# A count scan whose zero operand lies in PSUM, and a result store moved back in the queue of loads

## The chip, the cores and the metric

The kernel runs on one core of a Trainium2 chip. Times are device microseconds of one whole execution; lower is better. A profile gives the *span* of one profiled execution, which in these runs is mostly 1.8 to 2.3 us shorter than the time of the same execution. So times are compared with times here, and spans with spans.

## The reference

```python
# x: 8 x 2048 x 4096, w: 4096 x 1, float32
proj = (x @ w).squeeze(-1)
cm = np.maximum.accumulate(proj, axis=1)
is_record = (proj >= cm).astype(np.float32)
return np.cumsum(is_record, axis=1)
```

A projection of 16384 rows, and for each of 8 batches a running maximum, a compare and a running count over 2048 positions. The input is 268 MB, the output 64 KB.

## The kernel before

Positions 0 to 1919 are handled in five groups of 384 positions for all 8 batches (the loop); the last 128 positions form the *last batch*, which is cut into rows and smaller pieces so that little is left to do when the last data land. VectorE multiplies and sums columns 0 to 2815 of each row, GpSimd multiplies the remaining 1280 columns, and ScalarE sums GpSimd's products. TensorE transposes the sums into the tile `ps` in PSUM, and VectorE runs three instructions on them, the scans. The kernel places its tiles in two memories, SBUF and PSUM: `ps` and `w_v` lie in PSUM, the other tiles in SBUF. A *dot* below is one VectorE instruction that multiplies a row by w and sums.

```python
    ends = cut(2)                                   # two columns of an SBUF tile
    neg, zero = ends[:B, 0:1], ends[:B, 1:2]
    ...
    def scans(cm_, rec_, cnt_, n, cm0, cnt0):
        V.tensor_tensor_scan(                       # running maximum: PSUM and SBUF
            out=cm_, data0=ps[:B, :n], data1=neg.to_broadcast([B, n]), initial=cm0,
            op0=ALU.max, op1=ALU.max,
        )._wait_ge(psr, 1).then_inc(psr, 1)
        V.tensor_tensor(                            # compare: PSUM and SBUF
            out=rec_, in0=ps[:B, :n], in1=cm_, op=ALU.is_ge
        )._wait_ge(psr, 2).then_inc(psr, 1)
        V.tensor_tensor_scan(                       # count: SBUF and SBUF
            out=cnt_, data0=rec_, data1=zero.to_broadcast([B, n]), initial=cnt0,
            op0=ALU.add, op1=ALU.add,
        )._wait_ge(psr, 3).then_inc(cs, 1)
    ...
        for m, b in enumerate(rows):                # last batch: six rows ...
            row_load(m, 0, D, b, xt[m])
            if m == 3:                              # result of the fifth group
                SY.dma_start(
                    out=out[:, (NG - 1) * N : S0], in_=cnt
                )._wait_ge(cs, NG).then_inc(oe, 16)
        for i, (b, c0, c1, _, _) in enumerate(PIECES):   # ... and eight pieces
            row_load(B - 1 - b, c0, c1, b, xq[i])
    ...
        def piece(xb, v, p, dst_v, dst_p, landed):
            dot(xb[:, v[0] : v[1]], w_v[:, v[0] : v[1]], dst_v)._wait_ge(
                landed, 16).then_inc(sd, 1)         # VectorE, w in PSUM
            ...
            if p:
                xl = xb[:, p[0] : p[1]]
                G.tensor_mul(out=xl, in0=xl, in1=w_pool(*p))._wait_ge(
                    landed, 16).then_inc(pl, 1)     # GpSimd, both inputs in SBUF
                add_up(xl, dst_p)._wait_ge(pl, npool).then_inc(pa, 1)   # ScalarE
```

All loads and stores of x and the result are issued in program order by one queue (SyncE), so a store that waits holds up every load behind it (in the profile below a store waits for 36.9 us and is issued at 602.74, and the next load at 603.09). GpSimd does not take part in the scans: when it has finished its part of the fifth group it goes on to the last batch, while VectorE still has the fifth group's scans to do.

## Time and profile before

| | before |
|---|---|
| median of the first three timed runs | 632.62 us (632.54, 634.55, 632.62) |
| the profiled execution | 635.03 us, span 632.9 us |
| DMA | 90% busy or more in 39 of 40 slices, mean 424 GB/s |
| VectorE, GpSimd busy | 64%, 58% |
| fifth count scan | 3.74 us (the other four: 1.005 us) |

Loads bound most of the span. The change concerns the last 35 us. This is the timeline of the kernel before around the fifth group's scans and at the last dot. Columns: start in us, length in us, engine, source line, operation, output<-input, shapes, count, and in brackets the idle time before it with what ended it. DVE is VectorE, POOL is GpSimd, PE is TensorE, ACT is ScalarE, and SPq is the queue of loads and stores.

```profile
...
595.93 2.90 POOL L285 TENSOR_TENSOR xall<-xall,w_sb 128x1280 f32<-128x1280 f32 x1
...
597.35 1.00 DVE L132 TENSOR_TENSOR_SCAN cm<-ps,cm,small 8x384 f32<-8x384 f32 x1 [3.58 <-PE ps L264]
...
598.97 3.74 DVE L139 TENSOR_TENSOR_SCAN cnt<-rec,cnt,small 8x384 f32<-8x384 f32 x1
598.99 2.91 POOL L285 TENSOR_TENSOR xall<-xall,w_sb 128x1280 f32<-128x1280 f32 x1 [0.17 <-DMA xall<-in_x_dram]
...
602.64 3.05 DVE L117 CUSTOM_DVE_ANT_0 xall<-xall,w_v 128x2816 f32<-128x2816 f32 x1
602.74 0.31 SPq L183 DMA_DIRECT2D out_dram<-cnt  x1
603.09 2.96 SPq L173 DMA_DIRECT2D xall<-in_x_dram  x6
...
626.86 0.54 DVE L117 CUSTOM_DVE_ANT_0 xall<-xall,w_v 128x384 f32<-128x384 f32 x1
...
628.69 0.47 DVE L132 TENSOR_TENSOR_SCAN cm_l<-ps,cm,small 8x128 f32<-8x128 f32 x1 [1.29 <-PE ps L315]
...
```

The maximum scan (597.35), with one input in PSUM, runs beside a GpSimd multiply and takes its usual 1.00 us. The count scan (598.97), with two inputs in SBUF, starts ahead of the next multiply and ends only after it (602.71 against 601.90). The first dot of the last batch (602.64), the store (602.74) and the next loads (603.09) all come behind that scan. The interval from the last dot to the last maximum scan (1.29 us idle) is TensorE's.

The next two fences are of the kernel before as well: the DMA queue's own waits (total, times, longest), and the busy time by engine in windows of 1 us (after the window and its width: TensorE, its weight loads, VectorE, ScalarE and GpSimd, with the number of instructions; the last three columns are TensorE's granted clock, the DMA share and GB/s).

```profile
...
SPq L183 <- DVE cnt L139: 36.9, 1, 36.9
...
```

```profile
...
601.00:602.00 1.00, 0.00 (x0) 0.00 (x0) 1.00 (x1) 0.07 (x1) 0.90 (x1) 0.51 1.03 442
602.00:603.00 1.00, 0.00 (x0) 0.00 (x0) 1.00 (x2) 1.00 (x1) 0.00 (x0) 0.50 0.54 229
603.00:604.00 1.00, 0.00 (x0) 0.00 (x0) 1.00 (x1) 0.30 (x2) 0.17 (x1) 0.50 0.06 12
604.00:605.00 1.00, 0.00 (x0) 0.00 (x0) 1.00 (x1) 0.00 (x0) 1.00 (x1) 0.50 1.43 262
605.00:606.00 1.00, 0.00 (x0) 0.00 (x0) 1.00 (x3) 0.00 (x0) 1.00 (x1) 0.50 0.66 229
...
```

The store holds the queue for 36.9 us; the loads in front of it run out between 602 and 603, and the rate falls to 12 GB/s.

### The profile page before, as it was taken

How to read it: one execution, taken by the hardware profiler on the slowest of the kernel's cores; microseconds unless marked ns; L12 is line 12 of the kernel's file. 1: busy time of each engine (PE TensorE's matmuls, PEld its weight loads, DVE VectorE, ACT ScalarE, POOL GpSimd, SP SyncE). 2: the span in 40 equal slices, each digit the busy share in tenths (PEclk: the TensorE clock that was granted, in tenths of full speed). 3: DMA queues.
4: the chain of work that ended last, by engine and by line, in shares of the span. 5: the costliest groups of instructions: out<-in, count | busy, mean ns of one | idle time of the engine just before them, and what ended most of it. 6: DMA issues, size and time to landing. Idle time of an engine off the chain costs nothing.

```text
span 632.9 us, 1226 instructions
## 1 busy us (share of the span) xinstructions
PE 32.4 (5%) x98; PEld 14.8 (2%) x98; DVE 406.2 (64%) x288; ACT 177.7 (28%) x262; POOL 369.4 (58%) x137
## 2 busy tenths in 40 slices
PE   7100000010000001000000000000001000000103
PEld 3000000000000000000000000000000000000001
DVE  0556666677655567766666575666667765556797
ACT  1322223222322222232323222222322232222422
POOL 0555666656555555666665555566665655556954
PEclk9999999985555556555555565555556555555656
DMA  9999999999999999999999999999999999999995
GB/s 380 419 441 438 435 423 444 430 429 438 438 432 423 444 435 432 429 444 429 423 444 441 426 426 444 432 436 429 444 429 426 441 435 435 423 447 410 433 364 203
DMA packets 7891, 268.55 MB, mean 424 GB/s; under 512 B 920, under 2 KB 1352, under 8 KB 1872
## 3 DMA queue, kind: packets, MB, share of 16 engines
q1 hardware_dynamic: 7872, 268.50, 98.4%
q10 hardware_dynamic: 16, 0.02, 0.0%
q8 instruction: 1, 0.02, 0.0%
q14 instruction: 2, 0.02, 0.0%
HBM read 268.45 MB, written 0.07 MB: 424 GB/s over the span
## 4 chain that ended last, share of the span: by engine, by line
POOL 52%; issue 39%; DVE 4%; PE 3%; DMA 0%; POOLq 0%; ACT 0%; DVEq 0%; ACTq 0%; SPq 0%
POOL xall L243 52%; DVE xall L117 3%; PE w_v L203 2%; PE ps L315 1%; DMA w<-in_w_dram 0%; PE ps L264 0%; PE ps L203 0%; POOLq L246 0%; DVE cm L132 0%; ACT w L213 0%; DVE rec L136 0%; DVE cm_l L132 0%; DVE cnt_l L139 0%; DVE rec_l L136 0%; POOLq L238 0%
## 5 line engine op out<-in xcount | busy, mean ns | idle before, releaser
L117 DVE CUSTOM_DVE_ANT_0 xall<-xall,w_v 128x2816 f32<-128x2816 f32 (+3 forms) x134 | 388.7, 2951 | 203.0 <-DVEq L225 203.0
L243 POOL TENSOR_TENSOR xall<-xall,w_sb 128x1280 f32<-128x1280 f32 x120 | 345.4, 2905 | 245.7 <-POOLq L246 245.7
L123 ACT ACTIVATE xall<-xall 128x1280 f32<-128x1280 f32 x129 | 162.6, 1261 | 431.7 <-POOL xall L243 411.9
L264 PE MATMUL ps<-identity,small 128*8 128x128 f32 x60 | 13.6, 418 | 565.9 <-ACT xall L123 565.9
L285 POOL TENSOR_TENSOR xall<-xall,w_sb 128x1280 f32<-128x1280 f32 (+1 forms) x8 | 22.1, 2763 | 8.7 <-DMA xall<-in_x_dram 8.7
L123 ACT ACTIVATION_READ_ACCUMULATOR xall<-xall 128x1 f32 x129 | 24.0, 186 | 0.0
L264 PEld LDWEIGHTS ps<-identity,small 128*8 128x8 f32 x60 | 7.4, 129 | 573.3 <-ACT xall L123 569.5
L132 DVE TENSOR_TENSOR_SCAN cm<-ps,cm,small 8x384 f32<-8x384 f32 x5 | 5.0, 1004 | 17.9 <-PE ps L264 17.9
L203 PE MATMUL w_v<-w,identity 8*128 8x512 f32 x14 | 12.1, 1056 | 0.0
L117 DVE DVE_READ_ACCUMULATOR2_ANT small<- 128x1 f32 x134 | 10.7, 80 | 0.0
L139 DVE TENSOR_TENSOR_SCAN cnt<-rec,cnt,small 8x384 f32<-8x384 f32 x5 | 7.8, 1553 | 0.2
L315 PE MATMUL ps<-identity,small 128*1 128x128 f32 (+1 forms) x22 | 4.8, 403 | 26.6 <-DVE small L117 26.6
L203 PEld LDWEIGHTS w_v<-w,identity 8*128 8x128 f32 x14 | 4.6, 332 | 7.3 <-issue 7.3
L210 ACT COPY w_sb<-w_v 128x768 f32<-128x768 f32 x1 | 0.8, 799 | 11.4 <-PE w_v L203 11.4
L315 PEld LDWEIGHTS ps<-identity,small 128*1 128x1 f32 (+1 forms) x22 | 2.3, 113 | 29.3 <-DVE small L117 28.1
L136 DVE TENSOR_TENSOR rec<-ps,cm 8x384 f32<-8x384 f32 x5 | 2.7, 546 | 0.2
L203 PE MATMUL ps<-w,identity 8*128 8x512 f32 x2 | 2.1, 1136 | 3.7 <-DMA w<-in_w_dram 3.7
L209 ACT ACT_TABLE_LOAD x1 | 1.3, 1283 | 1.6 <-SPq L145 1.6
L209 ACT COPY w_sb<-ps 128x512 f32<-128x512 f32 x1 | 0.6, 586 | 3.0 <-PE ps L203 3.0
L132 DVE TENSOR_TENSOR_SCAN cm_l<-ps,cm,small 8x128 f32<-8x128 f32 x1 | 0.5, 471 | 1.3 <-PE ps L315 1.3
L217 DVE MEMSET cm<- 8x384 f32 x1 | 0.4, 378 | 1.1 <-SPq L145 1.1
L285 POOL TENSOR_TENSOR xall<-xall,w 128x320 f32<-128x320 f32 x1 | 0.9, 866 | 0.0
(13 smaller groups left out, 3.6 us busy)
## 6 DMA issues: line engine op xcount, KB each, us to landing
xall<-in_x_dram SPq DMA_DIRECT2D x40, 6144.0 KB, 47.8
xall<-in_x_dram SPq DMA_DIRECT2D x6, 2048.0 KB, 38.2
xall<-in_x_dram SPq DMA_DIRECT2D x1, 1344.0 KB, 14.8
xall<-in_x_dram SPq DMA_DIRECT2D x2, 384.0 KB, 17.5
xall<-in_x_dram SPq DMA_DIRECT2D x1, 704.0 KB, 16.1
xall<-in_x_dram SPq DMA_DIRECT2D x1, 640.0 KB, 16.9
xall<-in_x_dram SPq DMA_DIRECT2D x2, 224.0 KB, 17.9
xall<-in_x_dram SPq DMA_DIRECT2D x1, 192.0 KB, 17.9
```

The source lines that it names most:

```text
L117: return V.tensor_tensor_reduce(out=xsl, in0=xsl, in1=wsl, scale=1.0, scalar=0.0, op0=ALU.mult, op1=ALU.add, accum_out=dst,)
L123: return A.activation(out=xsl, in_=xsl, func=ACTF.Copy, accum_out=dst)
L132: V.tensor_tensor_scan(out=cm_, data0=ps[:B, :n], data1=neg.to_broadcast([B, n]), initial=cm0, op0=ALU.max, op1=ALU.max,)._wait_ge(psr, 1) ...
L136: V.tensor_tensor(out=rec_, in0=ps[:B, :n], in1=cm_, op=ALU.is_ge)._wait_ge(psr, 2).then_inc(psr, 1)
L139: V.tensor_tensor_scan(out=cnt_, data0=rec_, data1=zero.to_broadcast([B, n]), initial=cnt0, op0=ALU.add, op1=ALU.add,)._wait_ge(psr, 3).th ...
L203: i = T.matmul(out=dst, lhsT=identity[:NW, k : k + 1].to_broadcast([NW, P]), rhs=w_row, start=True, stop=True,).then_inc(bw, 1)
L209: A.copy(out=w_sb[:, CV - VC :], in_=ps)._wait_ge(bw, 1).then_inc(wc, 1)
L210: A.copy(out=w_sb[:, : CV - VC], in_=w_v[:, VC:CV])._wait_ge(bw, NW).then_inc(wc, 1)
L243: i = G.tensor_mul(out=xl, in0=xl, in1=w_sb).then_inc(pl, 1)
L264: i = T.matmul(out=ps[:B, j:N:R], lhsT=l[:, j * B : (j + 1) * B], rhs=identity, start=k == 0, stop=k == 1,)
L285: G.tensor_mul(out=xl, in0=xl, in1=w_pool(*p))._wait_ge(landed, 16).then_inc(pl, 1)
L315: i = T.matmul(out=ps[:m, :P], lhsT=l[:, :m], rhs=identity, start=k == 0, stop=k == len(parts) - 1,)
```

## The change

The intent: bring the count scan beside GpSimd's multiply from 3.74 us to the 1.00 us that the maximum scan takes there, and keep the store from holding up the loads of the last batch.

```diff
-    ends = cut(2)
-    neg, zero = ends[:B, 0:1], ends[:B, 1:2]
+    neg = cut(1)[:B]
+    zero = ps[:B, WC - 1 :]
@@
             row_load(m, 0, D, b, xt[m])
-            if m == 3:
+        for i, (b, c0, c1, _, _) in enumerate(PIECES):
+            row_load(B - 1 - b, c0, c1, b, xq[i])
+            if i == 3:
                 SY.dma_start(
                     out=out[:, (NG - 1) * N : S0], in_=cnt
                 )._wait_ge(cs, NG).then_inc(oe, 16)
-        for i, (b, c0, c1, _, _) in enumerate(PIECES):
-            row_load(B - 1 - b, c0, c1, b, xq[i])
@@
         V.wait_ge(wc, 3)
+        V.memset(zero, 0.0)
         with V.Fori(0, NG):
```

The last column of `ps` is free by then: its one earlier use, for spreading w at the start, has been copied out (`wc`), and the transposes write columns 0 to 383 at most.

## The prediction

> **What bounds the kernel now.** The page shows the DMA engines 90% busy or more in 39 of 40 slices, at a mean 424 GB/s: loads are the limit for most of the span, and the change leaves them alone. The last 35 us differ. In the timeline, the fifth group's count scan runs from 598.97 to 602.71: 3.74 us, where the other four groups' take 1.005 us. GpSimd runs a multiply from 598.99 to 601.90. VectorE starts the last batch's first dot at 602.64, and from there the chain of waits is VectorE without a gap (dots of 3.0 us) until 627.4, then TensorE, the last scans and the store. Three rows had landed by 598.99 (GpSimd starts on the third), so VectorE was late, not the data.
>
> The queue of loads stops there too: its waits show 36.9 us on the store, which needs that scan. It issues at 602.74, the next load at 603.09. In windows of 1 us, DMA moves 229, 12, 262 and 229 GB/s from 602 to 606, against about 430: some 2.3 us of transfer lost.
>
> **Why the scan is slow.** [...] 3.744 us against 1.005 us. The max scan of the same group has one operand in PSUM, runs beside a GpSimd multiply (597.35), and takes 1.00 us as always.
>
> **What the change does.**
> - Zero in PSUM: the count scan has one SBUF input. I expect about 1.0 us, so 2.7 us less, directly on the critical path. The other scans gain nothing (GpSimd idle).
> - Added: an 8x1 memset at the start, about 0.1 us, hidden behind queued loads.
> - Store moved: rows 5 and 6 and pieces 1 to 4 are issued from 566 to 583, not after 603. The 2.3 us transfer gap goes. When the store's wait ends (about 600), over 15 us of loads are still queued, so the last four pieces aren't late.
>
> **On the critical path.** VectorE's chain starts 2.7 us earlier, at about 599.95. The final pieces landed about 1.4 us before VectorE reached them (estimate from GpSimd's data-released starts, 615.58, 618.79, 622.08, and sizes); they move 2.3 us earlier, so VectorE stays behind the data by about 1 us, to 624.7. The tail is unchanged. Either half alone: the scan would give nearly all (the store's wait then ends at 600, before the queued loads run out at 602.7); the moved store almost nothing, since VectorE would still start at 602.64. The parts don't add up: both lift the same stall.
>
> **Prediction.** 632.62 - 2.7 = **629.9 us**, range 629.2 to 631.3. Faster by over 2%: 0.005; within 2%: 0.99; slower: 0.005.
>
> **What would show it right or wrong.**
> - Fifth count scan: 1.0 us, not over 3.
> - First dot of the last batch at about 600.0; no idle VectorE up to 624.7.
> - No dip of DMA rate from 602 to 606; last loads done by about 622.7 instead of 625.
> - The store's issue near 600.3, and the DMA queue's wait on it about 17 us.
>
> **What would make it wrong.** [...] The store's small writes could hold the last pieces back by more than VectorE lags; then VectorE waits between dots and the gain falls towards 2 us. TensorE's clock in the tail could shift by tenths. Run-to-run scatter (632.54 to 634.55) is nearly as large as the effect.

What it rests on is the trace: beside a multiply the count scan took 3.74 us, the maximum scan, with one input in PSUM, 1.00 us. That the count scan would follow with its zero in PSUM was my estimate. The sum: 632.62 - 2.7 = 629.9 us, where 2.7 is 3.74 less the 1.0 expected.

## The result, and the profile after

| | before | after |
|---|---|---|
| median | 632.58 us (4 runs, 631.75 to 634.55) | 631.59 us (4 runs, 631.52 to 632.39) |
| ratio, 95% interval | | 0.9983 (0.9958 to 1.0007) |
| span of the profiled execution | 632.9 us | 629.4 us |
| time of the profiled execution | 635.03 us | 631.60 us |
| fifth count scan | 3.74 us | 1.00 us |

A ratio is the mean time of one kernel's fast runs over that of the other's of the same rounds, so it is not quite the ratio of the medians. 631.59 us lies above the predicted range of 629.2 to 631.3. All outputs are right.

The lines of the timeline of the changed kernel that answer to those of before:

```profile
...
597.21 1.00 DVE L132 TENSOR_TENSOR_SCAN cm<-ps,cm,small 8x384 f32<-8x384 f32 x1 [3.60 <-PE ps L265]
...
598.83 1.00 DVE L139 TENSOR_TENSOR_SCAN cnt<-rec,cnt,ps 8x384 f32<-8x384 f32 x1
598.90 2.90 POOL L286 TENSOR_TENSOR xall<-xall,w_sb 128x1280 f32<-128x1280 f32 x1 [0.21 <-DMA xall<-in_x_dram]
599.76 3.05 DVE L117 CUSTOM_DVE_ANT_0 xall<-xall,w_v 128x2816 f32<-128x2816 f32 x1
599.86 0.31 SPq L185 DMA_DIRECT2D out_dram<-cnt  x1
...
600.21 6.63 SPq L173 DMA_DIRECT2D xall<-in_x_dram  x4
...
623.98 0.54 DVE L117 CUSTOM_DVE_ANT_0 xall<-xall,w_v 128x384 f32<-128x384 f32 x1
...
625.22 0.47 DVE L132 TENSOR_TENSOR_SCAN cm_l<-ps,cm,small 8x128 f32<-8x128 f32 x1 [0.69 <-PE ps L316]
...
```

And of the changed kernel the DMA queue's wait on the store, and the same windows:

```profile
...
SPq L185 <- DVE cnt L139: 10.0, 1, 10.0
...
```

```profile
...
601.00:602.00 1.00, 0.00 (x0) 0.00 (x0) 1.00 (x1) 0.17 (x1) 0.80 (x1) 1.00 1.07 459
602.00:603.00 1.00, 0.00 (x0) 0.00 (x0) 1.00 (x3) 1.00 (x1) 0.00 (x0) 1.00 1.00 426
603.00:604.00 1.00, 0.00 (x0) 0.00 (x0) 1.00 (x1) 0.19 (x2) 0.25 (x1) 1.00 0.99 426
604.00:605.00 1.00, 0.00 (x0) 0.00 (x0) 1.00 (x1) 0.00 (x0) 1.00 (x1) 1.00 1.03 442
605.00:606.00 1.00, 0.00 (x0) 0.00 (x0) 1.00 (x3) 0.00 (x0) 1.00 (x1) 1.00 0.92 393
...
```

Between the two *profiles* the main points went as predicted: the first dot is 2.88 us earlier (602.64 to 599.76), the dip of the DMA rate is gone, the store leaves at 599.86. The spans differ by 3.5 us: 2.9 us of this is the earlier start, 0.6 us the shorter stretch after the last dot (1.29 to 0.69 us). Yet the *medians* differ by 1.0 us only, and the interval of the ratio does not exclude that there is no difference. So the first thing to ask is which executions were compared: the profiled execution of before took 635.03 us, and the median of before is 632.6. (*Before* stands for the kernel before from here on.)

### The profile page after: what moved, and what is told of

Read it like the earlier page. It is cut to its first block, busy times and chain, and to the rows that moved or that the text cites. A ratio compares the mean times of both kernels' runs of the same rounds, so it can differ in the third digit from the quotient of the medians.

```text
span 629.4 us, 1227 instructions
## 1 busy us (share of the span) xinstructions
PE 31.8 (5%) x98; PEld 14.4 (2%) x98; DVE 403.6 (64%) x289; ACT 177.8 (28%) x262; POOL 369.1 (59%) x137
## 4 chain that ended last, share of the span: by engine, by line
POOL 53%; issue 39%; DVE 4%; PE 3%; DMA 0%; POOLq 0%; ACT 0%; DVEq 0%; ACTq 0%; SPq 0%
POOL xall L244 53%; DVE xall L117 3%; PE w_v L203 2%; PE ps L316 1%; PE ps L265 0%; PE ps L203 0%; DMA w<-in_w_dram 0%; DVE cm L132 0%; POOLq L247 0%; ACT w L213 0%; DVE rec L136 0%; DVE cm_l L132 0%; DVE cnt_l L139 0%; DVE rec_l L136 0%; POOLq L239 0%
## 5 line engine op out<-in xcount | busy, mean ns | idle before, releaser
L139 DVE TENSOR_TENSOR_SCAN cnt<-rec,cnt,ps 8x384 f32<-8x384 f32 x5 | 5.0, 1001 | 0.2
```

The lines of the kernel that those rows point to most:

```text
L139: V.tensor_tensor_scan(out=cnt_, data0=rec_, data1=zero.to_broadcast([B, n]), initial=cnt0, op0=ALU.add, op1=ALU.add,)._wait_ge(psr, 3).th ...
```

## The experiments

**Theory A, the race.** The stall is real, but most executions of before don't have it. Count scan and multiply start within tens of nanoseconds of each other (20 ns in the first profile), and which of them goes first differs from execution to execution. **Theory B.** Every execution of before is stalled, and the changed kernel loses its gain elsewhere; the profiled execution of before was longer for another reason, such as TensorE's granted clock of 0.62.

The executions, sorted (us; three chips, here called X, Y and Z; runs of one chip are to be compared). What follows rests on clusters of times 2 to 3 us apart and on the traces:

| kernel | chip | times |
|---|---|---|
| before | X | 631.67 631.68 631.81 631.86 631.90 631.99 632.14 632.45 632.75 |
| before once more | X | 631.83 631.97 632.02 632.22 632.62 |
| scan only | X | 631.97 631.97 632.01 632.07 632.29 |
| forced collision, before | X | 633.24 633.88 634.05 634.25 634.46 |
| kept apart, before | X | 632.03 632.21 632.21 632.23 632.43 |
| before | Y | 631.72 631.81 632.12 632.18 632.26 632.37 632.46 632.47 634.68 635.19 635.30 635.42 |
| changed kernel once more | Y | 631.60 631.82 631.88 632.11 632.39 632.43 |
| store only | Y | 631.68 631.87 632.15 632.33 632.36 632.47 |
| forced collision, changed | Y | 631.81 632.15 632.39 632.43 632.56 632.71 |
| small delay, before | Y | 632.26 632.43 632.52 632.64 632.64 634.76 |
| small delay, changed | Y | 631.61 631.88 632.18 632.27 632.42 632.48 |
| warm TensorE, changed | Y | 631.65 631.78 631.83 631.84 631.98 632.26 |
| rebalanced | Y | 630.45 630.76 630.82 631.59 631.59 632.37 |
| rebalanced, mended | Y | 630.98 631.00 631.02 631.03 631.09 632.74 |
| before | Z | 631.53 631.77 632.15 632.36 632.40 632.59 632.60 632.61 632.70 633.15 635.13 |
| larger delay, before | Z | 634.11 634.91 635.10 635.12 635.27 635.32 |
| larger delay, changed | Z | 631.70 631.95 631.97 631.99 632.20 632.72 |

### Before once more

No edit: the kernel before was submitted as it is, for a second profile.

> The kernel before, unchanged, to see how its executions scatter. Theory A (the race): in the first profile the count scan started at 598.97 and GpSimd's multiply at 598.99, 20 ns apart[...]. The profiled execution took 635.03 us, the timed median was 632.62, so it was one of the bad ones. A expects times in two clusters about 2.7 us apart, near 631.8 to 632.6 and near 634.5 to 635, and a profile whose fifth count scan takes either 1.0 us (span about 630) or 3.7 us (span about 632.5). Theory B (the stall is in every execution; the first profile was longer because TensorE's clock was at 0.62, and the changed kernel loses its gain in something else): the scan takes 3.7 us whatever the time, also in an execution near 632.

The profile fell on an execution of 632.22 us (span 630.1). Of this second profile of the kernel before, the timeline:

```profile
...
598.91 1.00 DVE L139 TENSOR_TENSOR_SCAN cnt<-rec,cnt,small 8x384 f32<-8x384 f32 x1
598.99 3.63 POOL L285 TENSOR_TENSOR xall<-xall,w_sb 128x1280 f32<-128x1280 f32 x1 [0.23 <-DMA xall<-in_x_dram]
599.84 3.05 DVE L117 CUSTOM_DVE_ANT_0 xall<-xall,w_v 128x2816 f32<-128x2816 f32 x1
...
```

The same kernel, and the roles are swapped: here the scan starts 80 ns ahead, takes 1.00 us, and the *multiply* takes 3.63 us in place of 2.90. GpSimd is then still idle for 1.22 us until its next row lands and starts on it at 603.84, as in the first profile (603.83), so its 0.73 us cost nothing. Theory B falls: this execution of before holds no stall of VectorE. The two expected clusters did not both appear on this chip: all 14 executions of before on X are below 633.

### One half of the change at a time

Scan only: the zero in PSUM and its memset, the store left behind the fourth row.

```diff
-    neg, zero = ends[:B, 0:1], ends[:B, 1:2]
+    neg = cut(1)[:B]
+    zero = ps[:B, WC - 1 :]
@@
+        V.memset(zero, 0.0)
```

> Only the zero operand in PSUM, the store where it was. Theory A: the scan is never stalled, no execution above 633, mean the same as the changed kernel's, 631.6; against before a gain of 0 to 1.5 us, which is the share of before's executions that are stalled times 2.7. Theory B: the scan is 1.0 us and the gain is the same small one as with both parts, or 2.7 us if it was the moved store that gave time back.

632.01 us median, ratio to before 1.0 (0.9987 to 1.0014), scan 1.00 us. On this chip before was never stalled, so there was nothing to gain.

Store only: the store behind the fourth piece, the zero in SBUF.

```diff
-            if m == 3:
-                SY.dma_start(out=out[:, (NG - 1) * N : S0], in_=cnt)._wait_ge(cs, NG) ...
@@
             row_load(B - 1 - b, c0, c1, b, xq[i])
+            if i == 3:
+                SY.dma_start(out=out[:, (NG - 1) * N : S0], in_=cnt)._wait_ge(cs, NG) ...
```

> Only the store moved, zero in SBUF. Theory A: same as before within 0.3 us; if the profile falls on a bad execution, a scan of 2.9 to 3.7 us, no dip of the DMA rate, yet the last batch still starts late and the time is 634. Theory C: 0.4 us or more below before.

632.24 us median. The eight unstalled executions of before on this chip have a mean of 632.17 us, this kernel's mean is 632.14. So the moved store gives nothing where the scan isn't late. What it would give in a stalled execution was not seen: the six executions here hold none.

The changed kernel was run once more beside it.

> The changed kernel once more. So far: before again had a scan of 1.005 us beside a GpSimd multiply stretched to 3.63 us, and 632.0; scan only 632.0; forced collision 634.05; kept apart 632.2. Theory A (the collision costs some 2 us[...]) expects the changed kernel equal to before within 0.3 us here, unless before is hit in some rounds. The shorter tail of its first profile (0.69 us from the last dot to the max scan, against 1.2 to 1.5 in the others) I take for scatter of TensorE's speed: expected here either way, 631.4 with it and 632.0 without. Rival theory C: the moved store does shorten something by 0.5 us in every execution, so it is below before and below scan only by 0.4 us or more in all rounds.

Its mean is 632.04 us, 0.13 us below that of before's unstalled executions on the same chip and well within the scatter; theory C (0.4 us from the moved store in every execution) falls. Before's four other executions on this chip, 634.68 to 635.42, have a mean of 635.15 us, 2.97 us above its unstalled ones. The changed kernel shows none such. TensorE's granted clock, which theory B blamed, does not sort them: two of these four have a mean clock of 1.0 over the execution, and three of the unstalled eight (631.81, 632.12, 632.18) one of 0.61 to 0.62.

### The collision forced, and taken away

GpSimd gets one multiply more, on data that nobody uses any longer, which starts right after the second row's and so ahead of the count scan.

```diff
         for m, b in enumerate(rows):
+            if m == 2:
+                G.tensor_mul(
+                    out=xbuf[NS - 1][:, VC:D], in0=w_sb, in1=w_sb
+                )._wait_ge(pa, 1)
             piece(
```

> The kernel before with one more 128x1280 multiply on GpSimd (about 2.9 us, result unused) between the second and third row of the last batch, which starts about 0.14 us ahead of the count scan in every execution, so that the collision is forced. Theory A: all executions like the bad ones: scan about 3.7 us, times 634.4 to 635, some 2 us or more above before's median. Theory B: before is stalled already in every execution, so its median does not change by more than 0.3 us.

Timeline of before with the extra multiply (L294):

```profile
...
598.73 2.33 POOL L294 TENSOR_TENSOR xall<-w_sb 128x1280 f32<-128x1280 f32 x1
...
598.93 2.94 DVE L139 TENSOR_TENSOR_SCAN cnt<-rec,cnt,small 8x384 f32<-8x384 f32 x1
...
601.80 3.05 DVE L117 CUSTOM_DVE_ANT_0 xall<-xall,w_v 128x2816 f32<-128x2816 f32 x1
...
```

All five executions are slow, mean 633.98 us against 632.03 of before on this chip: 1.9 us, and the scan takes 1.94 us longer than its 1.00. The multiply was shorter than I expected (2.33 us), so the scan lost less than the 2.7 us of the first profile, and the times lie below the 634.4 to 635 that I expected. In these runs a stall of the scan thus costs about its own length; that all five have it is read from their times, since one was profiled.

The same multiply in the changed kernel:

> The changed kernel with the same extra GpSimd multiply that forced the collision in before. Theory A: the scan takes 1.0 us although the multiply starts ahead of it, and the time is that of the changed kernel within 0.3 us, 1.7 to 2.3 us below forced before (634.05). [...]

The other outcome: a scan of 2.9 us and about 634 us.

```profile
...
598.75 2.33 POOL L295 TENSOR_TENSOR xall<-w_sb 128x1280 f32<-128x1280 f32 x1
...
598.94 1.00 DVE L139 TENSOR_TENSOR_SCAN cnt<-rec,cnt,ps 8x384 f32<-8x384 f32 x1
599.87 3.05 DVE L117 CUSTOM_DVE_ANT_0 xall<-xall,w_v 128x2816 f32<-128x2816 f32 x1
...
```

With the zero in PSUM the scan runs through the middle of the multiply in 1.00 us (2.94 us with it in SBUF), and the multiply takes 2.33 us in both. Mean 632.34 us, 0.30 us above the changed kernel's, and 1.64 us below forced before (1.7 to 2.3 expected; the two ran on different chips, X and Y). So of the 1.9 us above, up to 0.3 may be the extra multiply's own. This pair of traces shows what the change counts on: with the zero in PSUM the count scan doesn't wait for the multiply.

The other way round, before with GpSimd's third multiply held until the scan has ended:

```diff
         for m, b in enumerate(rows):
+            if m == 2:
+                G.wait_ge(cs, NG)
             piece(
```

> The kernel before, but GpSimd's multiply of the third row of the last batch waits until the fifth count scan has ended, so they can't collide. GpSimd loses about 1 us there and has some 2 us of idle time after it. Theory A: scan 1.0 us in every execution, times like the changed kernel's, 631.6, none above 633. Theory B: 2.7 us below before's median, about 630.

Scan 1.00 us, all executions between 632.03 and 632.43 us: without a collision before is within 0.2 us of the changed kernel (mean 632.22 against 632.04 on Y), with its zero in SBUF and its store in the old place. Theory B had expected 630 us; theory A's 631.6, taken from the first runs of the changed kernel, was 0.4 to 0.8 too low. As before had no stalled execution on this chip, this run does not show a stall taken away.

### Why only some executions: delaying the scan

If start order decides, a small delay of the scan should turn most executions into stalled ones. A first attempt put one memset ahead of each group's count scan:

```diff
+        if n == N:
+            V.memset(cnt_l[:, :64], 0.0)
         V.tensor_tensor_scan(
             out=cnt_,
```

> The kernel before with one 8x64 memset on VectorE (about 0.1 us, its result unused) right ahead of each group's count scan. In the traces so far GpSimd's multiply starts 20 ns after the scan in the one stalled execution of before and 80 ns after it in the two where the scan was first. Theory A (a race decided by tens of ns): with the scan about 0.1 us later GpSimd wins in nearly every execution, so nearly all are at 634.5 to 635.5, scan 3.7 us; before itself has about 1 stalled execution in 5. If the outcome has another cause, the delay costs 0.1 us only and the share stays as in before.

> The same memset in the changed kernel. Theory A: there is nothing to race for, so all executions within 0.3 us of the changed kernel (631.5 to 632.6), scan 1.0 us.

One of six executions was stalled (634.76), not nearly all. The expectation failed, and so did the edit. The timeline of before with the small delay:

```profile
...
598.50 0.55 DVE L136 TENSOR_TENSOR rec<-ps,cm 8x384 f32<-8x384 f32 x1
...
599.00 0.11 DVE L140 MEMSET cnt_l<- 8x64 f32 x1
599.08 1.00 DVE L141 TENSOR_TENSOR_SCAN cnt<-rec,cnt,small 8x384 f32<-8x384 f32 x1
599.15 3.63 POOL L287 TENSOR_TENSOR xall<-xall,w_sb 128x1280 f32<-128x1280 f32 x1 [0.21 <-DMA xall<-in_x_dram]
...
```

The scan starts 0.58 us after the compare does, as it did without the memset (0.58 to 0.59 us in the first two profiles): the memset was hidden and delayed nothing. The control in the changed kernel, at 631.61 to 632.48 us, says no more than that the memset is harmless. The second attempt uses two larger memsets:

```diff
+        if n == N:
+            V.memset(cnt_l, 0.0)
+            V.memset(rec_l, 0.0)
         V.tensor_tensor_scan(
             out=cnt_,
```

> The kernel before with two 8x128 memsets on VectorE ahead of each group's count scan, which should start it 0.2 to 0.3 us later than its 0.58 us after the compare, hence after GpSimd's multiply, which starts 20 to 80 ns after the scan in the traces without them. Theory A[...]: every execution is stalled, scan over 3 us, all at 634.6 to 635.8. If start order does not decide, about 1 execution in 5 is stalled, the others are at 632.0 to 632.7.

> The same two memsets in the changed kernel: no stall, scan 1.0 us, only the delay itself, 0.3 us: 631.8 to 632.7.

Timeline of before with the larger delay:

```profile
...
599.30 2.90 POOL L288 TENSOR_TENSOR xall<-xall,w_sb 128x1280 f32<-128x1280 f32 x1 [0.21 <-DMA xall<-in_x_dram]
599.31 0.17 DVE L141 MEMSET rec_l<- 8x128 f32 x1
599.40 3.61 DVE L142 TENSOR_TENSOR_SCAN cnt<-rec,cnt,small 8x384 f32<-8x384 f32 x1
...
602.94 3.05 DVE L117 CUSTOM_DVE_ANT_0 xall<-xall,w_v 128x2816 f32<-128x2816 f32 x1
...
```

The scan now starts 0.10 us after the multiply, and all six executions are stalled, by their times (one was profiled): 634.11 to 635.32 us (634.6 to 635.8 expected), mean 634.97, where the ten unstalled executions of before on the same chip have a mean of 632.39. The same memsets in the changed kernel cost nothing visible (mean 632.09): in its profile the multiply starts 0.12 us ahead of the scan, and the scan takes 0.88 us. The scan was delayed by about 0.17 us only (0.75 us after the compare in place of 0.58), less than I had expected, and that turned 1 stalled execution in 11 into 6 in 6.

### The scatter at the end, and a version meant to beat both

The unstalled executions still scatter by some 0.8 us, and the first profile of the changed kernel had an unusually short stretch after its last dot: 0.69 us idle, where the profiles of before, of before once more and of scan only have 1.29, 1.37 and 1.48 us. To test whether TensorE's speed in its last burst is the cause (my theory), eight unused matmuls were put in front of its last burst, in the changed kernel:

```diff
+        for k in range(8):
+            i = T.matmul(out=ps[:B, P : 2 * P], lhsT=identity[:, :B], rhs=identity,
+                         start=True, stop=True)
+            if k == 0:
+                i._wait_ge(sd, len(rows))
         for k, (m, l, wait) in enumerate(parts):
```

> The changed kernel with 8 matmuls more (results unused) on TensorE after the sixth row's dot. From the last dot to the max scan it took 0.69, 0.98, 1.2, 1.3, 1.37 or 1.48 us in the profiles so far, and the executions without a stall scatter by 0.8 us; [...] If so, with TensorE kept busy ahead of it, that stretch is 0.7 us or less in all executions, which lie within 0.3 us of each other at about 631.3. If the scatter has another source, the range stays 631.5 to 632.4.

From the timeline of this kernel:

```profile
...
625.41 0.47 DVE L132 TENSOR_TENSOR_SCAN cm_l<-ps,cm,small 8x128 f32<-8x128 f32 x1 [0.69 <-PE ps L323]
...
```

The stretch is the short one in the profile, the median 631.84 us (changed kernel on this chip: 632.00). But the executions still spread over 0.6 us, twice what I expected, and the median is 0.5 us above what I expected. TensorE's speed explains part of the scatter at most, and that part is not shown; the rest stays open.

The rebalanced version gives GpSimd 256 columns more in each of the last batch's six rows, since VectorE had started late and GpSimd idles between rows (in the changed kernel's first profile for 6.7 us in all before six of its multiplies in the last batch, until data land):

```diff
+    VT = 2560
@@
-                slot(m)[1], (0, VC), (VC, D), st_v[:, b : b + 1], st_p[:, b : b + 1],
+                slot(m)[1], (0, VT), (VT, D), st_v[:, b : b + 1], st_p[:, b : b + 1],
```

The diff is cut: GpSimd's second copy of w and its split multiplies are left out, and so are two changes of the pieces' columns, and the order of TensorE's last matmuls.

> A version meant to beat both. In the profiles without a stall VectorE reaches the last piece about 1.2 us after its data have landed, as its dots (3.0 us a row) started late; GpSimd idles 2 us a row. Here 256 columns of each of the last batch's six rows go from VectorE to GpSimd (second copy of w placed there), and the GpSimd parts' matmuls are moved ahead of the last one. Expected: dots of the rows 2.75 us, VectorE waiting for data from the first piece on, the last dot ending about 1.2 us sooner, time about 1.0 to 1.4 us below the changed kernel.

631.20 us median; 0.8 us below the changed kernel where I expected 1.0 to 1.4. Its last dot started at 624.15, no sooner than in the changed kernel run on that chip (624.12): I had also moved the fifth piece wholly to VectorE, and it landed at 622.2, behind which VectorE then had 2.5 us to do. The mended version splits that piece again (512 columns on VectorE, 256 on GpSimd) and adds the eight matmuls (both diffs are against the changed kernel, and this one is cut in the same way):

```diff
-        (0, 1280, 2048, (1280, 2048), None),
+        (0, 1280, 2048, (1536, 2048), (1280, 1536)),
@@
+        for k in range(8):
+            i = T.matmul(out=ps[:B, P : 2 * P], lhsT=identity[:, :B], rhs=identity, ...)
```

> The better version mended: its last dot ended no sooner than the changed kernel's, because the fifth piece then lay wholly on VectorE and everything behind its landing waited. Here that piece is split again (512 columns VectorE, 256 GpSimd), the rows keep 2560 columns on VectorE, and the 8 extra matmuls keep TensorE busy. Expected: last dot ends 0.4 us sooner than the changed kernel's, tail 0.5 us shorter, 630.3 to 631.0 in all executions.

Timeline of the mended version:

```profile
...
624.00 0.55 DVE L119 CUSTOM_DVE_ANT_0 xall<-xall,w_v 128x384 f32<-128x384 f32 x1
...
625.03 0.47 DVE L136 TENSOR_TENSOR_SCAN cm_l<-ps,cm,small 8x128 f32<-8x128 f32 x1 [0.47 <-PE ps L333]
...
```

631.03 us median, five of six executions within 0.11 us of each other, and one at 632.74 (not explained); two of the six lie in the expected 630.3 to 631.0. Its ratio to before is 0.9969 (0.9943 to 0.9996), that of the unmended version 0.9967 (0.9940 to 0.9993); by the mean the two can't be told apart, by the median the mended one is ahead, and both medians lie below the changed kernel's on this chip (632.00 us; the mended one ran later). These are differences of 0.1 to 0.2%, and the ratios to before include its stalled executions. The last dot is only 0.12 us sooner than in the changed kernel's second profile (0.4 expected), since VectorE now waits for data at the fourth and fifth pieces. Of the 1.0 us between the two profiled spans (628.8 and 629.8) this is 0.1, the shorter end 0.5 (0.47 us idle against 0.98), and the rest lies behind the issue of the last store (626.34 here, 626.95 there), which nothing here explains.

## Why the prediction was wrong

**The step that failed** is the sum: "632.62 - 2.7 = **629.9 us**". It took the stall of one profiled execution off the median of other executions, in which it mostly wasn't. The stall's size was about right (2.7 us predicted, 2.97 us between before's two clusters on chip Y), and so was its place on the critical path. What was wrong is "directly on the critical path" read as "in every execution": 0.99 us was measured between the medians, and the interval of the ratio (0.9958 to 1.0007) does not exclude a gain of zero.

How often is it there? Of the 42 executions of the unchanged kernel 7 took more than 634 us: 2 of 5 in the first measurements, 0 of 14 on X, 4 of 12 on Y, 1 of 11 on Z (633.15 there, between the clusters, is counted as unstalled). Of the 34 executions of the changed kernel (10 as it is, 24 with the extra multiply, memsets or matmuls) none took more than 632.72 us. Only two of the 42 were profiled with the scan in view (one of each kind); the others are sorted by their time alone. An estimate from these: 7/42 of 2.97 us is 0.5 us of mean, and almost nothing of the median, because the median is an unstalled execution. This is why a change that removes 2.7 us from a profile is worth 0.0 to 1.2 us in the comparisons here (ratios of 1.0 for the scan alone on X, 0.9981 for the whole change on Y), depending on how many bad executions before happened to have.

**It could have been seen beforehand.** The profiled execution took 635.03 us, 2.4 us more than the median of the timed ones, nearly the whole predicted gain. And count scan and multiply started 20 ns apart. Both numbers were on the table.

Point by point:

- "Fifth count scan: 1.0 us, not over 3": right in the profile; forced collision in both kernels shows 2.94 against 1.00 us.
- "First dot of the last batch at about 600.0; no idle VectorE up to 624.7": right (599.76; the last dot ends at 624.5).
- "No dip of DMA rate from 602 to 606; last loads done by about 622.7": right; the rate is 393 to 459 GB/s there, and falls to 3 GB/s in the window that starts at 623.
- "The store's issue near 600.3, and the DMA queue's wait on it about 17 us": issue right (599.86), wait wrong, 10.0 us. The four pieces ahead of it, issued from 579.92, took 9.9 us to issue, where I had reckoned with about 3.
- "the scan would give nearly all [...] the moved store almost nothing": not shown as put. Without a stall each half alone gives nothing, which the runs show; the moved store by itself in a stalled execution was not seen. That the old place of the store costs nothing once the scan is on time is shown by the kernel kept apart (mean within 0.2 us of the changed kernel's).
- "The tail is unchanged": not in the profile (1.29 to 0.69 us), but that is scatter: the changed kernel's second profile has 0.98 us.
- "Run-to-run scatter (632.54 to 634.55) is nearly as large as the effect": this was noticed and not followed up. The scatter *was* the effect.

Start order goes with the outcome where the starts are clearly apart (both inputs of the scan in SBUF): scan first by 70 to 80 ns, the multiply takes 3.62 to 3.63 us; multiply first by 0.10 to 0.20 us, the scan takes 2.94 to 3.61 us; and 0.17 us of delay turned one outcome into the other in all executions. The first profile, where the scan is recorded 20 ns ahead and yet waits (3.74 us), is the exception: at 20 ns the recorded starts did not show who would wait. In all three profiles with a stalled scan it ends 0.81 us after the multiply. By itself it takes 1.00 us, so it had some 0.2 us behind it before it was held up (an estimate from these two numbers). In the profile the instruction that waits is shown as started and busy (3.74 us for a scan of 1.00, 3.63 us for a multiply of 2.90), not as idle. Why the start times differ between executions is not shown; the multiply is released by a load's landing (0.17 us idle before it in the stalled profile, 0.23 us in the other; in the forced kernels, where the row has landed by the time of this multiply, there is no idle time), so jitter of the landing is the likely source, argued only.

For the scatter at the end I had TensorE's speed in mind. The last burst's single-column matmuls had a mean of 344 ns in the changed kernel's first profile (0.69 us idle) and 398 to 415 ns in those of before, of before once more and of scan only (1.29, 1.37 and 1.48 us). But the recorded clock does not agree: it is 1.00 all through the burst in the changed kernel's first profile and just as much in that of before once more, its mean over the execution of scan only is 1.0, and in the windows of before it is 0.50 up to 628. Its mean over the execution of the changed kernel's second profile (0.98 us idle) is 0.622. The warm version shows the short stretch in its one profile, yet its executions spread over 0.6 us. So this cause of the scatter is not shown.

## What to carry to other kernels

Before a stall seen in a profile is subtracted from a median, compare the time of the profiled execution with the other executions: if it is longer by about the stall (here 2.4 of 2.7 us), the stall may be a feature of that execution, and the mean gain is then its frequency times its size. Where two instructions, one of which was seen to wait for the other, start within tens of nanoseconds of each other (here 20 to 80), suspect two clusters of times, and test it by delaying one of them for certain, looking in the trace that the delay took place. Removing such a stall still pays: it takes away the slow cluster (here 7 of 42 executions above 634 us, and none of 34 after) even where the median doesn't move.
